# Layer 0's settings on GpSimd, its first heads later, and five smaller moves in a two-layer decoder trunk

## The chip, the cores and the metric

The kernel runs on one core of one Trainium2 chip. The core has TensorE (PE, with the weight load PEld shown apart), VectorE (DVE), ScalarE (ACT), GpSimd (POOL) and SyncE (SP, which issues most of the transfers). The metric is the device time of one execution in microseconds (us). Before the change it is 1268.68 us, the median of 3 runs (1268.33 to 1268.9).

## The reference

Two layers of a decoder trunk work on 512 tokens behind 16 learned meta tokens (528 columns), with a width of 1024, in float32. Each layer normalises, makes one projection for two groups of heads, transforms each group, joins them, projects back and adds; a SwiGLU block of width 2816 follows. Cut to what matters:

```python
def hybrid_layer(h, ...):
    xn = rmsnorm(h, attn_norm_g)
    fq, fk, fv, flog, rq, rk, rv, rg = split(xn @ w_in)
    logf = log_sigmoid(flog + b_fgate)                  # forget gates
    fox_out = fox_attention(fq, fk, fv, logf)           # 8 heads of 64:
        # c = cumsum(logf); softmax(q.k/8 + c[t] - c[s], s <= t) @ v
    rq, rk = rotate(rq), rotate(rk) / sqrt(128)
    ret = retention_chunkwise(rq, rk, rv)               # 4 heads of 128:
        # o_t = sum over s <= t of gamma^(t-s) (q_t.k_s) v_s
    ret = head_groupnorm(ret, ret_gn_g)                 # mean and variance of a head
    mix = concat([fox_out, silu(rg) * ret])
    h = h + mix @ w_out
    hn = rmsnorm(h, ffn_norm_g)
    return h + (silu(hn @ w_gate) * (hn @ w_up)) @ w_down
# after two layers: rmsnorm, and the 16 meta tokens are dropped
```

## The kernel before, in words

**Layout.** Activations lie transposed: 8 tiles of 128 features by 528 columns. A product in float32 is made of three matmuls on rounded parts: each weight tile is cast on ScalarE (whi, line 199), the remainder is subtracted on GpSimd or VectorE (wlo, line 202), the activations have xh and xl (lines 327 and 328), and TensorE adds whi·xh, whi·xl and wlo·xh in a bank (line 225). One such group for one of the 8 tiles is a "dense step": six matmuls of 264 columns in layer 0 (two halves of 528). Later results are split in the same way on ScalarE and VectorE (lines 150 and 151).

**Stages.** Layer 0's start fills fixed parts of tiles (`enter_att`, with `zero`, lines 91 and 122): one rows of the query tiles qo, zero rows of the key tiles kc, of the forget sums fs, the scores pr, the values pd, and small tiles pm and re. TensorE runs nine matmuls on ones until the first weights are there. Then come the norm of the layer, the first heads' projections, and the heads: four pairs of attention heads (`fox`) and four retention heads (`ret`, called hd 0 to 3).

An attention pair goes through scores (line 524: kc·qo with the forget sums in the same tile, and kx·qs), a masked maximum (line 528, nmax), the exponential on ScalarE (line 541), transposes on TensorE (line 427) into pth and ptl, and the product with the values (lines 586 and 594), which ScalarE and VectorE bring back with the sums (lines 588, 589, 597 and 598, into mixt).

A retention head goes through its values (transposed on TensorE, mean and centred values sq in lines 690 and 691, then rvh and rvl), rotated queries and keys (rqh, rql, rkh, rkl), scores (line 727), a product with the decay (line 732, sd), rounding into rsh and rsl, the product with the values (lines 758 and 761), the norm over the head (`col_rstd`: matmuls on ones in line 298, Ln and Exp in lines 303 and 304, one Newton step in lines 305 to 308) and the gate. For hd 0 and 1 the gate's silu is made from exponentials, which begins with a maximum with −80 (line 664, ge); for hd 2 and 3 it is the activation itself, whose table ScalarE must load (lines 416 and 418).

**Order.** TensorE's order is written out: a plan of steps, in which dense steps are the base, and the heads' steps are merged in at places counted in dense steps. `spread(main, a, b)` puts an attention pair's steps evenly between two places; `ret_places` takes ten numbers for a retention head's steps (the first for the values, the fourth and fifth for the first product and the third group of scores). The other engines' orders are made by a scheduler which keeps the dependencies; `pin` keeps a piece of work in the order of the program, `tc.high_priority()` lets it go ahead, and `tc.issue_after(x)` holds it behind x. Every engine carries out its own queue in order. Two tables of banks serve the matmuls: psd, and psa, whose banks a reader must leave before the next matmul takes them.

**The end.** The last norm works on two halves of columns. In the second half (`square_b`, `sum_b`, `after_7`) the squares of the 8 tiles are made on ScalarE (line 1140), six of them are added on VectorE (line 1143), and TensorE adds the sum and the last two squares by matmuls on ones (line 1169). Ln, Exp, a Newton step, the scaling and the last transfers follow.

Of the kernel before, what the change touches and what calls it, by code (L numbers as in the profile page):

```python
# [13 lines left out]
ALU = mybir.AluOpType  # L14
# [25 lines left out]
def hybrid_kernel(ctx, tc, x_t, w_in, w_fl, w_out, w_gate, w_up, w_down, vecs, b_fg, rope, decay, mask, ident, out_t):  # L40
# [42 lines left out]
    def enter_att(l):  # L83
# [37 lines left out]
    def zero(l, t):  # L121
        (nc.gpsimd if l else nc.vector).memset(t, 0.0)  # L122

# [166 lines left out]

    def col_rstd(parts, n, cols, rname, pinned=False):

# [6 lines left out]
        with tc.high_priority():  # L299
            r = tt(rname)  # L300
            a = tt("nwt")
            for v, (c0, c1) in zip(views, cols):
                pin(nc.scalar.activation(r[:, c0:c1], v, AF.Ln, bias=epsc, scale=1.0 / n), pinned)
            pin(nc.scalar.activation(r[:, c_all], r[:, c_all], AF.Exp, scale=-0.5), pinned)
            nc.vector.tensor_mul(a[:, c_all], r[:, c_all], r[:, c_all])
            for v, (c0, c1) in zip(views, cols):
                nc.vector.scalar_tensor_tensor(a[:, c0:c1], v, n * EPS, a[:, c0:c1], ALU.add, ALU.mult)
            nc.vector.scalar_tensor_tensor(r[:, c_all], a[:, c_all], 3.0 * n, r[:, c_all], ALU.subtract, ALU.mult)
# [6 lines left out]
    def pin(f, pinned=True):  # L315
        if pinned:
            tc.keep_in_program_order(f)

    def scale_split(st, gcol, cols, then=None):
# [3 lines left out]
        for k in range(NK):  # L323
            xh = state.tile([128, T], F32R, name=f"xh{k}", tag=f"xh{k}")
            xl = state.tile([128, T], F32R, name=f"xl{k}", tag=f"xl{k}")
            g = vcol(gcol + k)
            pin(nc.scalar.activation(xh[:, c], h[k][:, c], AF.Copy, scale=g), then)  # L327
            pin(nc.vector.scalar_tensor_tensor(xl[:, c], h[k][:, c], g, xh[:, c].bitcast(F32),  # L328
# [47 lines left out]
    def forget_gates(l, st):  # L376
# [251 lines left out]

    def ret_dense(l, hd, ly, real, st, which):
        QC = REAL if real else FULL  # L630
# [22 lines left out]
        def g_done(ps):  # L653
# [3 lines left out]
            if hd > 1:  # L657
                silu(sv(sg, real), LOGS)
                return
# [3 lines left out]
            x = sv(sg, real)  # L663
            nc.vector.scalar_tensor_tensor(u, x, -80.0, x, ALU.max, ALU.max)
            nc.scalar.activation(u, u, AF.Exp, scale=-1.0)
# [10 lines left out]
    def ret_steps(l, hd, st, real):  # L676
# [27 lines left out]
        def scores(grp):  # L704
# [26 lines left out]
            for kn, o, sc, dd in reads:  # L731
                nc.vector.tensor_mul(sd[0:kn, o], sc, dec[0:kn, dd])
# [92 lines left out]
    def ffn(l, st, real, last):  # L825
# [40 lines left out]
        def x_forms(k):  # L866
            def go():
# [4 lines left out]
                g0, g1 = vcol(V_FFN + l * NK + k), vcol(V_FFN + l * NK + HB + k)  # L872
                nc.scalar.activation(s[:, 0:2], two(h[k]), AF.Copy, scale=g0)
                nc.vector.tensor_sub(s[:, 2], s[:, 1], s[:, 0])
# [220 lines left out]
        else:  # L1095
# [34 lines left out]
            def square_b(m):  # L1130
                if m == 0:
                    t = fft("S", F32, (128, 6, w), 2)
                    fin["one"] = [t[:, i, 0:nb] for i in range(2)]
                    fin["acc"], fin["rb"], fin["tb"] = (t[:, i, 0:nb] for i in range(3, 6))
                    d = fin["acc"]
                elif m < NK - 2:
                    fin["sq", m] = d = tt("sq")[:, 0:nb]
                else:
                    d = fin["one"][m - NK + 2]
                pin(nc.scalar.activation(d, h[m][:, cb], AF.Square))  # L1140
# [111 lines left out]
    def layer(l):  # L1252
# [17 lines left out]
        def rd(hd, which):  # L1270
            return ret_dense(l, hd, ly, real, ret[hd], which)

# [42 lines left out]
        def first_parts():  # L1315
            ly["parts"] = col_parts(ly["acc"], FULL, True)
            convert(3, NK, True)
# [123 lines left out]
```

## Time and profile before

| | before |
|---|---|
| median of 3 runs | 1268.68 us |
| profiled execution | 1268.51 us |
| its span | 1266.7 us |
| TensorE busy | 1250.7 us (99%) |
| VectorE busy | 994.4 us (79%) |
| ScalarE busy | 706.2 us (56%) |
| GpSimd busy | 274.3 us (22%) |
| granted TensorE clock | 0.998 |

A row of a timeline gives the start, the duration, the engine, the line, the instruction, its output and inputs with their sizes, and in brackets how long the engine stood idle before it and what released it. "x2" is two instructions that follow each other. A row of the waits gives who waited for whom, the total in us, how many times, and the longest. The ends of matmuls are modelled, so times from start to start are used for TensorE where a tenth of a microsecond matters. A row of the stretches gives its limits and length, and for each engine the busy time and the number of instructions, then the granted clock, the transfers' share and GB/s.

### The profile page before, as it was taken

To read this page: it belongs to the slowest core of one execution; us is meant where nothing else is said; L and a number is where in the kernel's file an instruction comes from. 1 tells how busy PE (TensorE), PEld (TensorE's weight loads), DVE (VectorE), ACT (ScalarE), POOL (GpSimd) and SP (SyncE) were. 2 spreads that over 40 slices of the span, in tenths; PEclk is the share of its full clock that TensorE was granted. 3 is DMA by queue.
4 is the path that set the end of the run, shared out by engine and by line. 5 is a ranking of instruction groups with operands and counts; after the bars stand their busy time and mean duration, and the time that the engine had idled before them with its cause. 6 is when DMAs were issued, how large, how long until landed. Compare 5 with 4: busy or idle time off the path is not lost.

```text
span 1266.7 us, 23528 instructions
## 1 busy us (share of the span) xinstructions
PE 1250.7 (99%) x9223; PEld 1192.2 (94%) x9223; DVE 994.4 (79%) x1800; ACT 706.2 (56%) x1305; POOL 274.3 (22%) x540
## 2 busy tenths in 40 slices
PE   9999999999999999999999999999999999999997
PEld 9999999999999999999999989998789999999996
DVE  8887756879988888887786877567899888888867
ACT  7767655676444444444466665557764444444445
POOL 3555546420000000000126556554100000000000
PEclk9999999999999999999999999999999999999999
DMA  6212222223333333332322122222233333333321
GB/s 218 67 60 69 83 76 73 71 67 117 105 97 100 100 101 100 101 101 84 101 77 84 61 84 74 71 89 67 100 96 121 100 101 101 100 101 101 100 84 67
DMA packets 43342, 116.19 MB, mean 92 GB/s; under 512 B 5088, under 2 KB 12000, under 8 KB 43232
## 3 DMA queue, kind: packets, MB, share of 16 engines
q1 hardware_dynamic: 42800, 114.41, 28.1%
q8 instruction: 72, 1.18, 0.4%
q14 instruction: 38, 0.31, 0.1%
q10 hardware_dynamic: 432, 0.29, 0.1%
HBM read 112.58 MB, written 2.10 MB: 91 GB/s over the span
## 4 chain that ended last, share of the span: by engine, by line
PE 91%; DVE 4%; ACT 4%; issue 1%; DMA 0%; ACTq 0%; DVEq 0%
PE psd L225 28%; PE psa L912 18%; PE psd L1047 14%; PE psd L912 13%; PE psa L225 5%; PE psa L1047 4%; PE psa L427 2%; PE psa L524 1%; PE psa L594 1%; PE psa L761 1%; PE psa L727 1%; ACT whi L199 1%; PE psa L298 0%; ACT xh L327 0%; DMA raw<-w_in 0%
## 5 line engine op out<-in xcount | busy, mean ns | idle before, releaser
L202 POOL TENSOR_TENSOR wlo<-raw,whi 128x128 fp32r<-128x128 f32 x504 | 259.1, 548 | 256.0 <-ACT whi L199 235.3
L225 PE MATMUL psd<-xh,whi 128*128 128x264 f32 (+1 forms) x792 | 195.5, 314 | 0.0
L225 PE MATMUL psd<-xh,wlo 128*128 128x264 f32 (+1 forms) x792 | 186.9, 304 | 0.0
L225 PE MATMUL psd<-xl,whi 128*128 128x264 f32 (+1 forms) x792 | 186.4, 303 | 0.4 <-DVE xl L328 0.4
L225 PEld LDWEIGHTS psd<-xh,whi 128*128 128x128 f32 x792 | 128.5, 190 | 4.9 <-ACT whi L199 0.5
L225 PEld LDWEIGHTS psd<-xh,wlo 128*128 128x128 f32 x792 | 127.0, 188 | 6.3 <-DVE wlo L202 0.4
L225 PEld LDWEIGHTS psd<-xl,whi 128*128 128x128 f32 x792 | 127.6, 189 | 5.1 <-DVE xl L328 1.1
L199 ACT CAST whi<-raw 128x512 fp32r<-128x512 f32 (+1 forms) x168 | 97.9, 613 | 41.7 <-PE psd L225 28.6
L900 ACT CAST whi<-raw 128x1024 fp32r<-128x1024 f32 (+2 forms) x62 | 54.8, 885 | 51.2 <-PE psd L912 39.8
L900 ACT CAST fwhi<-raw 128x1024 fp32r<-128x1024 f32 (+2 forms) x62 | 55.6, 897 | 48.0 <-PE psd L912 40.5
L122 POOL MEMSET kc<- 64x528 f32 x2 | 1.1, 532 | 345.4 <-PE psa L912 345.4
L901 DVE TENSOR_TENSOR wlo<-raw,whi 128x1024 fp32r<-128x1024 f32 (+2 forms) x62 | 62.9, 1015 | 12.6 <-ACT whi L900 12.5
L901 DVE TENSOR_TENSOR fwlo<-raw,fwhi 128x1024 fp32r<-128x1024 f32 (+2 forms) x62 | 64.0, 1033 | 11.0 <-ACT fwhi L900 10.7
L912 PE MATMUL psa<-th,whi 128*128 128x264 f32 (+1 forms) x232 | 65.4, 282 | 0.0
L912 PE MATMUL psa<-th,wlo 128*128 128x264 f32 (+1 forms) x232 | 65.4, 282 | 0.0
L912 PE MATMUL psa<-tl,whi 128*128 128x264 f32 (+1 forms) x232 | 65.3, 282 | 0.0
L912 PE MATMUL psa<-th,fwhi 128*128 128x264 f32 (+1 forms) x224 | 63.4, 283 | 0.0
L912 PE MATMUL psa<-tl,fwhi 128*128 128x264 f32 (+1 forms) x224 | 63.3, 283 | 0.0
L912 PE MATMUL psa<-th,fwlo 128*128 128x264 f32 (+1 forms) x224 | 63.2, 282 | 0.0
L541 ACT ACTIVATE pr<-pr,nmax 128x144 f32<-128x144 f32 (+1 forms) x64 | 36.8, 575 | 44.4 <-DVE nmax L528 25.7
L900 ACT CAST fwhi<-S 128x1024 fp32r<-128x1024 f32 x20 | 21.0, 1049 | 68.6 <-PE psa L912 66.5
L978 ACT COPY e<-psa 128x264 f32<-128x264 f32 (+1 forms) x114 | 42.9, 376 | 28.3 <-PE psa L912 24.1
(368 smaller groups left out, 4044.8 us busy)
## 6 DMA issues: line engine op xcount, KB each, us to landing
raw<-w_in SPq DMA_DIRECT2D x54, 512.0 KB, 3.5
raw<-w_gate SPq DMA_DIRECT2D x44, 512.0 KB, 4.0
fraw<-w_up SPq DMA_DIRECT2D x38, 512.0 KB, 3.5
raw<-w_down SPq DMA_DIRECT2D x64, 256.0 KB, 2.9
raw<-w_out SPq DMA_DIRECT2D x16, 512.0 KB, 3.5
raw<-w_down SPq DMA_DIRECT2D x32, 192.0 KB, 2.5
raw<-w_up SPq DMA_DIRECT2D x6, 512.0 KB, 3.5
h<-x_t SPq DMA_DIRECT2D x8, 264.0 KB, 4.5
```

Source lines behind the costliest of these rows:

```text
L199: pin(nc.scalar.copy(hi, job["raw"][:, c0:c1]), pinned)
L202: pin(sub(lo[:, c:c + step], job["raw"][:, c0 + c:c0 + c + step], hi[:, c:c + step].bitcast(F32)), pinned)
L225: nc.tensor.matmul(ps[1][b][:, 0:c1 - c0], w[:, wk, :], x[:, c0:c1], start=(k == 0 and i == 0), stop=(k == n - 1 and i == 2))
L427: nc.tensor.transpose(ps[:, 128 * j:128 * j + 128], src[:, o:o + 128], idt)
L524: nc.tensor.matmul(sc[0:nq, 0:c1 - c0], qq[:, q0:q0 + nq], kk[:, c0:c1], start=(i == 0), stop=(i == 1))
L541: nc.scalar.activation(pr, pr, AF.Exp, bias=nmax[0:nq], scale=-1.0, accum_out=rsum)
L594: nc.tensor.matmul(po[:, c0:SEQ], v[:, j, :], pp[:, j, META + c0:T], start=(j == 0 and i == 0), stop=(j == 4))
L900: nc.scalar.copy(hi, src)
L901: nc.vector.tensor_sub(lo, src, hi.bitcast(F32))
L912: nc.tensor.matmul(bank()[:, 0:b.shape[-1]], a[:, o + k, :], b, start=(fresh and k == 0 and i == 0), stop=(k == n - 1 and i == 2), skip_gr ...
L978: nc.scalar.copy(self.t["e"][:, i], self.t["x"][:, 0:w])
L1047: nc.tensor.matmul(v[:, 0:c1 - c0], a[:, s * n + k, :], b[:, c0:c1], start=(k == 0 and i == 0), stop=(k == n - 1 and i == 2))
```

## The change

Seven things change:

1. The twelve settings of zeros and ones of layer 0 that stood on VectorE are made on GpSimd, as those of layer 1 already were.
2. Places: in the first group of heads, layer 0's first attention pair goes from 11 to 12 (its end from 32.5 to 33), hd 0's values from 13 to 17.5 and its first product from 37.5 to 38.6 (38.3 in layer 1); hd 3's fifth place, the third group of its scores, goes from 55.5 to 54.9.
3. The gate's maximum with −80 is a `tensor_scalar_max` on one input instead of a `scalar_tensor_tensor` that names the same tile twice.
4. In layer 0's third retention head (hd 2) the norm's sums are copied from their banks by ScalarE, and the Newton step reads the copy.
5. The rounded scores rsh and rsl have three buffers instead of two; hd 3's last rounding goes ahead with priority, and hd 2's silu is issued after it. The first norm's rounding is now written out in `first_rounding`, and a copy of the forget gates is issued after it.
6. In layer 1 the second normalised forms of the FFN's inputs (S, line 873) are issued after the last xh.
7. At the end three squares instead of two go to TensorE's sum, and VectorE's last addition falls away.

```diff
-            (nc.gpsimd if l else nc.vector).memset(q_tiles[s][rest].bitcast(F32), 1.0)
+            nc.gpsimd.memset(q_tiles[s][rest].bitcast(F32), 1.0)
...
     def zero(l, t):
-        (nc.gpsimd if l else nc.vector).memset(t, 0.0)
+        nc.gpsimd.memset(t, 0.0)
...
+    def first_rounding(st):
+        c = slice(0, T)
+        sh, sl = st["parts"] = tt("sqh", F32R), tt("sql", F32R)
+        st["rounding"] = pin(nc.scalar.copy(sh[:, c], st["acc"][:, c])).ins
+        pin(nc.vector.tensor_sub(sl[:, c], st["acc"][:, c], sh[:, c].bitcast(F32)))
...
             for v, (c0, c1) in zip(views, cols):
                 pin(nc.scalar.activation(r[:, c0:c1], v, AF.Ln, bias=epsc, scale=1.0 / n), pinned)
+            if aside:
+                t = tt("sq")
+                for v, (c0, c1) in zip(views, cols):
+                    nc.scalar.copy(t[:, c0:c1], v)
+                views, cols = [t[:, c_all]], [(cols[0][0], cols[-1][1])]
...
-                nc.scalar.copy(z2[:, c0:c1], ps[32:32 + FH, 0:c1 - c0])
+                with ExitStack() if l else tc.issue_after(st["rounding"]):
+                    nc.scalar.copy(z2[:, c0:c1], ps[32:32 + FH, 0:c1 - c0])
...
-                silu(sv(sg, real), LOGS)
+                with tc.issue_after(other["rounded"]) if hd == 2 else ExitStack():
+                    silu(sv(sg, real), LOGS)
...
-            nc.vector.scalar_tensor_tensor(u, x, -80.0, x, ALU.max, ALU.max)
+            nc.vector.tensor_scalar_max(u, x, -80.0)
...
-            sh = at("rsh", bufs=2)
-            sl = at("rsl", bufs=2)
+            sh = at("rsh", bufs=3)
+            sl = at("rsl", bufs=3)
             full = used if kn == 128 else used - n
-            split(sh[:, 0:full], sl[:, 0:full], sd[:, 0:full])
+            with tc.high_priority() if hd == RH - 1 and grp[0] == 2 else ExitStack():
+                st["rounded"] = nc.scalar.copy(sh[:, 0:full], sd[:, 0:full]).ins
+                nc.vector.tensor_sub(sl[:, 0:full], sd[:, 0:full], sh[:, 0:full].bitcast(F32))
...
-            r = col_rstd(st["parts"], 128, QC, "r")
+            r = col_rstd(st["parts"], 128, QC, "r", aside=hd == 2 and not real)
...
-                nc.scalar.activation(s[:, 0:2], two(h[k]), AF.Copy, scale=g0)
+                with tc.issue_after(st["scaled"].ins) if real else ExitStack():
+                    nc.scalar.activation(s[:, 0:2], two(h[k]), AF.Copy, scale=g0)
...
-                    fin["one"] = [t[:, i, 0:nb] for i in range(2)]
+                    fin["one"] = [t[:, i, 0:nb] for i in range(3)]
...
-                elif m < NK - 2:
+                elif m < NK - 3:
...
-                sum_b(5)
                 v = psum_a()[:, 0:nb]
-                sums(v, [fin["one"][0], fin["acc"], fin["one"][1]])
+                sums(v, [fin["one"][0], fin["acc"]] + fin["one"][1:])
...
-            m0, r0, places = (((7 if l else 11, 31 if l else 32.5), (34, 40.5), (13, 33.5, 35.5, 37.5, 39, 40.5, 43, 44, 47.5, 48)),
+            m0, r0, places = (((7 if l else 12, 31 if l else 33), (34, 40.5), (13 if l else 17.5, 33.5, 35.5, 38.3 if l else 38.6, 39, 40.5, 43, 44, 47.5, 48)),
...
-                      ret_places(3, 52, 45.5, 47.5, 57.5, 55.5, 58.5, 60, 64.1, 63, 64.2))
+                      ret_places(3, 52, 45.5, 47.5, 57.5, 54.9, 58.5, 60, 64.1, 63, 64.2))
```

How this moves the instructions shows in the engines' orders. Line numbers after the change are larger by 12 to 17 from `first_rounding` on (the scores' line 524 is 538, the max's 664 is 679).

TensorE, where the first attention pair of layer 0 begins. Before:

```order
L225 MATMUL psd<-xh_181,whi 128x264 x2
L225 MATMUL psd<-xl_182,whi 128x264 x2
L225 MATMUL psd<-xh_181,wlo 128x264 x2
L524 MATMUL psa<-kc_105,qo_103 16x16
L524 MATMUL psa<-kx_462,qs_453 16x16
L225 MATMUL psd<-xh_185,whi 128x264 x2
```

And with the change:

```order
L225 MATMUL psd<-xh_181,wlo 128x264 x2
L225 MATMUL psd<-xh_185,whi 128x264 x2
L225 MATMUL psd<-xl_186,whi 128x264 x2
L225 MATMUL psd<-xh_185,wlo 128x264 x2
L538 MATMUL psa<-kc_105,qo_103 16x16
L538 MATMUL psa<-kx_462,qs_453 16x16
```

One dense step (xh_185, xl_186) has moved ahead of the first scores.

VectorE, around the first head's max (ge) late in the first group of layer 0; sg is the gate's input, pr and nmax the scores' maxima of the attention pair, ptl the transposed scores' remainder, sd the retention scores with their decay. Before:

```order
L655 SCALAR_TENSOR_TENSOR sg<-psd,R 128x528
L528 ISA pr,nmax<-psa,msk 128x264
L528 ISA nmax 128x1
L528 ISA pr,nmax<-psa,msk 128x264
L528 ISA nmax 128x1
L664 SCALAR_TENSOR_TENSOR ge<-sg 128x528
L533 TENSOR_TENSOR nmax<-nmax 128x1
L151 TENSOR_TENSOR ptl<-psa,pth 128x128
L545 STREAM_TRANSPOSE pe<-pr 32x128
L549 RECIPROCAL sums<-sums 128x8
L732 TENSOR_TENSOR sd<-psa,dec 128x264 x2
```

And with the change:

```order
L542 ISA pr,nmax<-psa,msk 128x264
L542 ISA nmax 128x1
L542 ISA pr,nmax<-psa,msk 128x264
L542 ISA nmax 128x1
L669 SCALAR_TENSOR_TENSOR sg<-psd,R 128x528
L547 TENSOR_TENSOR nmax<-nmax 128x1
L151 TENSOR_TENSOR ptl<-psa,pth 128x128
L679 TENSOR_SCALAR ge<-sg 128x528
L559 STREAM_TRANSPOSE pe<-pr 32x128
L563 RECIPROCAL sums<-sums 128x8
L747 TENSOR_TENSOR sd<-psa,dec 128x264 x2
```

The max is another instruction, and the correction of the maxima and ptl stand ahead of it; sd still stands behind it.

ScalarE, at the norm of layer 0's third retention head; ol is an attention pair's product on its way to mixt, rkh a rotated key's rounded part. Before:

```order
L303 ACTIVATE r<-psa,epsc 128x264
L588 COPY ol<-psa 64x16
L303 ACTIVATE r<-psa,epsc 128x264
L568 CAST pth<-pm 16x16
L304 ACTIVATE r<-r 128x528
L150 CAST rkh<-tq 128x528
L597 COPY ol<-psa 64x512
```

And with the change:

```order
L309 ACTIVATE r<-psa,epsc 128x264 x2
L313 COPY sq<-psa 128x264 x2
L315 ACTIVATE r<-r 128x528
L602 COPY ol<-psa 64x16
L611 COPY ol<-psa 64x512
L150 CAST rkh<-tq 128x528
L582 CAST pth<-pm 16x16
```

The two copies are new, the copies of ol stay ahead of rkh, and rkh comes behind both of them instead of between them.

More of the change, by code (lines that the diff above doesn't have):

```diff
@@ L326, in scale_split @@
             g = vcol(gcol + k)
-            pin(nc.scalar.activation(xh[:, c], h[k][:, c], AF.Copy, scale=g), then)
+            st["scaled"] = nc.scalar.activation(xh[:, c], h[k][:, c], AF.Copy, scale=g)
+            pin(st["scaled"], then)
             pin(nc.vector.scalar_tensor_tensor(xl[:, c], h[k][:, c], g, xh[:, c].bitcast(F32),
@@ L627, in hybrid_kernel, with ret_dense @@
     KLEN = (128, 128, 128, 128, META)
-    def ret_dense(l, hd, ly, real, st, which):
+    def ret_dense(l, hd, ly, real, st, which, other):
         QC = REAL if real else FULL
@@ L1132, in square_b @@
                     t = fft("S", F32, (128, 6, w), 2)
[L1133 removed]
+                    fin["one"] = [t[:, i, 0:nb] for i in range(3)]
                     fin["acc"], fin["rb"], fin["tb"] = (t[:, i, 0:nb] for i in range(3, 6))
                     d = fin["acc"]
[L1136 removed]
+                elif m < NK - 3:
                     fin["sq", m] = d = tt("sq")[:, 0:nb]
                 else:
[L1139 removed]
+                    d = fin["one"][m - NK + 3]
                 pin(nc.scalar.activation(d, h[m][:, cb], AF.Square))
@@ L1270, in rd @@
         def rd(hd, which):
-            return ret_dense(l, hd, ly, real, ret[hd], which)
+            return ret_dense(l, hd, ly, real, ret[hd], which, ret[RH - 1])
         mixes = [[fox[0], ret[0], fox[1], ret[1]], [fox[2], ret[2], fox[3], ret[3]]]
```

5 lines of the change are left out of this document (3 added, 2 removed).

## The prediction

> **What bounds the kernel now.** I read the page first (busy times, then the chain that ended last), then the waits of TensorE, then its busy time by stretches, then the timeline around every wait of TensorE that these showed.
>
> ```profile
> PE 1250.7 (99%) x9223; PEld 1192.2 (94%) x9223; DVE 994.4 (79%) x1800; ACT 706.2 (56%) x1305; POOL 274.3 (22%) x540
> ...
> PE 91%; DVE 4%; ACT 4%; issue 1%; DMA 0%; ACTq 0%; DVEq 0%
> ```
>
> TensorE (PE) works 1250.7 us of a span of 1266.7. The other 4% + 4% of the chain are the places at which it stood still. The change touches no matmul but one, so it can only win back the remaining 16 us of idle time or add to them. The waits of TensorE name their pieces:
>
> ```profile
> PE psa L1283 <- DVE wide L62: 1.6, 1, 1.6
> PE psa L727 <- DVE ptl L151: 1.0, 1, 1.0
> PE psa L761 <- DVE rsl L151: 0.9, 3, 0.4
> PE psa L1169 <- ACT S L1140: 0.9, 1, 0.9
> PE psa L524 <- DVE kc L472: 0.8, 1, 0.8
> PE psa L594 <- DVE ptl L151: 0.7, 1, 0.7
> PE psa L524 <- DVE mixt L598: 0.7, 1, 0.7
> PE psa L427 <- DVE sd L732: 0.4, 1, 0.4
> PE psa L524 <- DVE sq L691: 0.4, 1, 0.4
> PE psd L225 <- DVE xl L328: 0.4, 1, 0.4
> PE psa L761 <- ACT rsh L150: 0.2, 1, 0.2
> PE psa L427 <- DVE nmax L528: 0.2, 1, 0.2
> ```
>
> Total us, times, longest: 8.2 us in fourteen waits; the rest of the 16 is the tail after the last matmul. By stretches (length, then busy time and count of PE, PEld, DVE, ACT, POOL, then clock):
>
> ```profile
> 36.00:75.00 39.00, 35.04 (x274) 33.04 (x273) 30.95 (x85) 25.66 (x68) 16.34 (x34) 1.00 0.19 65
> 75.00:230.00 155.00, 155.00 (x1268) 154.12 (x1266) 109.73 (x271) 97.61 (x239) 89.16 (x172) 1.00 0.23 74
> 230.00:265.00 35.00, 34.30 (x272) 33.57 (x271) 26.49 (x59) 25.47 (x54) 13.91 (x27) 1.00 0.19 61
> ```
>
> So 39.00 − 35.04 = 3.96 us of idle time lie between 36 and 75 us, where the first heads of layer 0 run. These are eight of the fourteen waits (kc, nmax, sq, product ptl, score ptl, sd, rsh, one rsl). A full stretch issues 1268 matmuls in 155 us, one every 0.122. A wait costs more than its idle time, since a matmul's end counts as busy:
>
> ```profile
> 36.40 0.40 PE L225 MATMUL psd<-xh,wlo 128*128 128x264 f32 x2
> 37.56 0.17 PE L524 MATMUL psa<-kc,qo 128*16 128x16 f32 x1 [0.76 <-DVE kc L472]
> ```
>
> The second matmul of that pair starts 0.122 after 36.40, the next one at 37.56: 1.04 where 0.12 is dense, a loss of 0.92 against 0.76 shown. I add 0.16 to each wait: 3.96 + 8 × 0.16 = 5.2 us are lost between 36 and 75.
>
> **The change part by part.** I take times from the profiled execution, 1268.51 us (span 1266.7 and 1.8 around it); the median of the runs is 1268.68, 0.17 more.
>
> Twelve settings on GpSimd. VectorE's queue loses them ahead of its first x form:
>
> ```profile
> 1.72 0.50 DVE L122 MEMSET kc<- 64x528 f32 x1 [0.16 <-issue]
> ...
> 5.53 0.73 DVE L328 SCALAR_TENSOR_TENSOR xl<-h,vec,xh 128x528 fp32r<-128x528 f32 x1
> ```
>
> The settings fill VectorE from 1.72 until 5.53, so xl comes up to 1 us sooner. Of that TensorE can use little, about 0.3 us: its first product waits for whi as well. And 0.3 us won there only lengthens the wait for kc, which ends at 37.41 (37.56 on TensorE) after a chain on ScalarE and VectorE. I count 0; the bounds are −0.3 and +0.3. GpSimd is free for them: its own few settings are short, and its subtractions start much later.
>
> First heads later. One dense step (6 matmuls of 264 columns, 6 × 0.122 = 0.73 us) goes ahead of the first scores, which wait for kc. At 37.56 TensorE has done 0.73 us more: +0.73. The values of the first retention head go from place 13 to 17.5, so the score that waited for the bank freed by sq L691 (0.4 + 0.16) and the transposes that waited for nmax (0.2 + 0.16) find theirs free: +0.9. But TensorE now comes 1.6 us sooner to the first transposes of pr and to the product that waits for ptl L151, while VectorE's row of score maxima, vv and the two passes over the values stays as long, only in another order. By VectorE's new order I lay the score maxima at about 47.2 where TensorE arrives at about 46.7, an estimate from the durations before: a new wait of 0.7. The product's wait (0.7 + 0.16) shrinks by about half: +0.4. Sum for 36 to 58 us: 0.73 + 0.9 − 0.7 + 0.4 = 1.3. Bounds: 0 (all is waited for again) and 0.73 + 0.9 + 0.9 = 2.5.
>
> The max of the gate, one input instead of two, and behind the first score correction:
>
> ```profile
> 62.55 3.72 DVE L664 SCALAR_TENSOR_TENSOR ge<-sg 128x528 f32<-128x528 f32 x1
> 66.19 0.15 DVE L533 TENSOR_TENSOR nmax<-nmax 128x1 f32<-128x1 f32 x1
> 66.26 0.28 DVE L151 TENSOR_TENSOR ptl<-psa,pth 128x128 fp32r<-128x128 f32 x1
> ...
> 68.13 1.20 DVE L732 TENSOR_TENSOR sd<-psa,dec 128x264 f32<-128x264 f32 x3
> ```
>
> ```profile
> 62.32 3.38 POOL L202 TENSOR_TENSOR wlo<-raw,whi 128x128 fp32r<-128x128 f32 x8
> ```
>
> ```profile
> L664 DVE SCALAR_TENSOR_TENSOR ge<-sg x4: 658/795/3722, 62.5 to 750.2; 128x528 f32<-128x528 f32 x2, 128x512 f32<-128x512 f32 x2
> ```
>
> ```profile
> L472 DVE TENSOR_SCALAR kc<-fs,pick x2: 490/535/580, 36.9 to 665.6; 40x528 fp32r<-40x528 f32 x2
> ```
>
> The first of four L664 took 3.72 us, against a shortest of 0.66. It started 0.23 after eight subtractions of GpSimd in a row and ended 0.57 after the last (65.70): it did not run beside them. Behind it stood nmax and ptl, which TensorE waited for (1.0 + 0.16), then sd (0.4 + 0.16), and through these rsh (0.2 + 0.16) and rsl ((0.9 − 0.4) / 2 = 0.25 of the row of three, + 0.16): 2.5 us together. In the new order nmax and ptl are issued before the max, and the max is a one-input instruction. Nearest row: L472, 0.49 to 0.58 on the same 528 columns; the other bound is 3.72 again. I take 0.5, since nothing with one tensor input stood as long in this trace: all four waits go, +2.5. If the max is held as long as before it costs what the second rival says.
>
> The Trainium skill bears on this, against the change. "SBUF — State Buffer", "SBUF: two separate sides", says that VectorE and GpSimd share one pair of ports as an exclusive lock for a whole instruction, and that VectorE asks for it with two SBUF inputs or in a two-port mode. The 3.72 beside the eight subtractions agrees. "VectorE: DVE Perf Modes", "Mode 2×_2P", gives the two-port mode to single-source fp32 instructions from SBUF; by it the new max would need the lock as well, which is the second rival's case. No run here shows that yet.
>
> Third norm's sums copied. Two ScalarE copies of 264 columns and one VectorE instruction of 528 in place of two:
>
> ```profile
> L978 ACT COPY e<-psa x114: 356/374/382, 324.0 to 1225.3; 128x264 f32<-128x264 f32 x57, 128x256 f32<-128x256 f32 x57
> ```
>
> ```profile
> L307 DVE SCALAR_TENSOR_TENSOR nwt<-psa,nwt x19: 413/432/692, 25.4 to 924.2; 128x264 f32<-128x264 f32 x14, 128x512 f32<-128x512 f32 x5
> ```
>
> ```profile
> 239.48 0.28 PE L524 MATMUL psa<-kx,qs 128*128 128x264 f32 x1
> 240.47 0.39 PE L524 MATMUL psa<-kc,qo 128*128 128x264 f32 x1 [0.70 <-DVE mixt L598]
> ```
>
> ```profile
> 239.74 0.67 DVE L598 TENSOR_TENSOR mixt<-psa,ol 64x512 f32<-64x512 f32 x1
> ```
>
> ```profile
> 234.37 4.88 POOL L202 TENSOR_TENSOR wlo<-raw,whi 128x128 fp32r<-128x128 f32 x8 [4.16 <-ACT whi L199]
> ```
>
> The scores at 240.47 waited 0.70 for a bank that L598 read until 240.41. With the sums copied, two banks of the norm are free when the second copy ends, some 2 × 0.374 after the norm's second Ln, at about 237.6, ahead of TensorE at 239.6; those scores stop waiting: 0.70 + 0.16 = 0.86. The copies and the reordering put rkh and rkl some 1.2 us later, and the products with them (L727, 241.54) would come 0.86 sooner: I lay rkl at about 241.0 against 240.7 and leave 0.35 of a wait. +0.5; bounds 0.9 and, if the new two-input instruction is held by GpSimd like L664, the third rival.
>
> Three buffers for rounded scores, and the last rounding of the fourth head with priority:
>
> ```profile
> 880.01 1.28 ACT L418 ACT_TABLE_LOAD   x1
> ...
> 882.29 0.54 ACT L150 CAST rsh<-sd 128x416 fp32r<-128x416 f32 x1
> ```
>
> In layer 1 this rounding stands behind two table loads of 1.28 and TensorE's earlier product, whose buffer it takes. It now goes first, so one wait for rsl of the three (0.4 + 0.16, at 882.9) goes: +0.56. What it is moved past is a whi cast, a silu and two mxh casts, each up to 0.9 later; mxh is used by TensorE some 4 us on. A second rsl wait (701 us, about 0.28 + 0.16) goes, because layer 1's first product stands one dense step later: +0.44.
>
> Layer 1's FFN start. Two casts stood ahead of the last x form's:
>
> ```profile
> 911.04 1.33 ACT L873 ACTIVATE S<-h,vec 128x512 f32<-128x512 f32 x2
> 912.28 0.71 ACT L327 ACTIVATE xh<-h,vec 128x512 fp32r<-128x512 f32 x1
> ```
>
> They are now issued behind it. That x form comes 1.3 us sooner and the wait for xl (0.4 + 0.16) goes: +0.56. The differences that read S begin only after eight subtractions on VectorE, so their delay is covered.
>
> The end. One VectorE addition of squares less, one pair of matmuls more.
>
> ```profile
> 1256.95 0.68 ACT L1140 ACTIVATE S<-h 128x240 f32<-128x240 f32 x2
> ```
>
> ```profile
> 1257.39 1.48 PE L1169 MATMUL psa<-S,ones 128*128 128x240 f32 x6 [0.89 <-ACT S L1140]
> ```
>
> Three pairs of matmuls took 1.48, so a further pair some 0.4. TensorE waited 0.89 for the first of these two squares; it can now start with the one before, some 0.6 sooner. +0.2, bounds −0.2 and +0.4.
>
> Sum: 1.3 + 2.5 + 0.5 + 0.56 + 0.44 + 0.56 + 0.2 = 6.1. 1268.51 − 6.1 = 1262.4; with the 0.17 of the median, **1262.6 us**. That the early gain is kept: from 75 to 230 TensorE is busy 155.00 of 155.00, with GpSimd at 89 and VectorE at 110, so nothing there is shorter of time than TensorE.
>
> **The rivals.**
>
> *The stage stays as long.* VectorE is busy 30.95 of the 39 us from 36 to 75, ScalarE 25.66, with waits between them; TensorE would only come sooner to the same results. For it: six of the eight waits there are for VectorE's results one after the other, and the change gives VectorE almost nothing to save but the max. Against it: the 3.1 us of the held L664 are themselves on that row. Then the 3.8 of this stage fall out, and 2.3 stay: 1266.4.
>
> *The max is held again.* The eight subtractions still follow one another for 3.4 us, now also around the max. Then sd, behind it, comes about 0.8 us earlier than 68.13 and no more, since ptl no longer waits for the max but sd does. Everything gained before is waited for there: 0.8 in place of 3.8, so 1268.5 − 0.8 − 2.3 + 0.2 = 1265.6. For it: the 3.72 us. Against it: the one-input rows of 0.49 to 0.58.
>
> *GpSimd's row holds VectorE at both new places, and the kernel gets slower.* L307's one-instruction form in the third norm now reads two SBUF inputs, sq and nwt, as L664 did; from the bank it took 0.41 to 0.69. Behind it in VectorE's queue stands rkl, for which TensorE waits. If it starts inside a row of eight subtractions like the one of 4.88 us that ended at 239.25, it stands up to 3.0 longer (3.72 − 0.7), with the 0.5 lost. With the second rival's loss: 1268.5 − 0.8 − 1.76 + 3.0 + 0.2 = 1269.1. It decides where more than 2.6 us of subtractions remain when that instruction starts. Against it: it starts at about 239.5, after that row's end.
>
> That the change doesn't do what it says: the new orders show every move, so I give this no share.
>
> **How the numbers follow.** My forecast, all waits but those named gone: 0.60. Max held again: 0.17. Stage as long: 0.13. Both held: 0.05. What I have not seen (a wait at a new place): 0.05, to both sides. The low end: all of 5.2 + 0.86 + 0.56 + 0.44 + 0.56 + 0.4 = 8.0 won, 1260.6, a little less for an earlier start: 1260.3. The high end takes in the first two rivals: 1266.6. The likeliest case alone spans 1260.3 to 1264. A measurement of this kernel tells 0.2%, 2.5 us, from no change: faster means below 1266.1. Forecast, held max and half of what is unseen: 0.79. Same: the unchanged stage and the third rival's smaller prices, 0.16. Slower: 0.05.
>
> **What would show it.** In the changed kernel's waits: ptl before L727 and sd gone, kc still there with 0.5 to 0.8, a wait for nmax at about 46 us; TensorE's busy time from 36 to 75 at least 37 of 39; the first max near 0.5 us; the score at 240 not waiting for L598; the fourth head's 416-column rounding before the table loads; the xl wait at 914 gone. The prediction is wrong if the max takes over 2 us, if 36 to 75 still shows over 3 us of idle time, or if a stretch that was full (75 to 230, 265 to 640, 930 to 1250) shows idle time.

## The result, and the profile after

The change takes 1261.31 us (median of 6 runs, 1261.24 to 1262.03) against 1268.58 before (6 runs, 1268.33 to 1268.9): 0.9944 of the time, 95% interval 0.9931 to 0.9956. That is 7.3 us less; 6.1 were forecast.

The page of the changed kernel, TensorE's share first and then the chain that ended last by engine:

```profile
PE 1248.7 (99%) x9225; PEld 1191.9 (95%) x9225; DVE 989.2 (79%) x1786; ACT 706.6 (56%) x1307; POOL 281.6 (22%) x552
...
PE 95%; DVE 3%; ACT 2%; DMA 0%; issue 0%; ACTq 0%; DVEq 0%
```

TensorE's share of the chain went from 91% to 95%. Its waits, in the same columns as before:

```profile
PE psa L1300 <- DVE wide L62: 1.6, 1, 1.6
PE psa L608 <- DVE ptl L151: 0.5, 1, 0.5
PE psa L1187 <- ACT S L1158: 0.2, 1, 0.2
PE psa L441 <- DVE nmax L542: 0.2, 1, 0.2
PE psd L225 <- DVE xl L341: 0.2, 1, 0.2
```

(Lines 538, 608, 1187 and 1300 are 524, 594, 1169 and 1283 of before; the offset goes from 6 in `col_rstd` to 18 at the end.) Fourteen waits have become five. The wait for kc is gone, as are the waits for sq, sd, rsh, rsl, mixt, and the score's wait for ptl. The wait for xl in this list is another one, at 7.7 us in the kernel's start; the one at 914 us (now 908) no longer shows. By stretches:

```profile
36.00:75.00 39.00, 38.21 (x307) 37.25 (x306) 32.87 (x91) 29.48 (x78) 20.05 (x39) 1.00 0.21 69
...
230.00:265.00 35.00, 34.91 (x277) 34.14 (x277) 28.70 (x60) 25.83 (x52) 16.72 (x32) 1.00 0.14 46
```

Between 36 and 75 us TensorE issues 307 matmuls, where it issued 274. The stretch from 930 to 1250, full before, now has 0.21 us of idle time: the wait for S, which has moved ahead of 1250 with the end. Taken from start to start (the time between two matmuls over that of a dense row), the 7.1 us by which the span is shorter come from these places:

| place | lost before, us | lost after, us | gain, us | forecast, us |
|---|---|---|---|---|
| first scores (kc), with the dense step done ahead | 37.56 | 37.26, and 0.73 of work more | 1.03 | 0.73 |
| 40 to 58 us (nmax, sq, product) | 0.36 + 0.60 + 0.96 | 0.36 + 0.78 | 0.78 | 0.6 |
| 65 to 71 us (ptl, sd, rsh, rsl) | 1.13 + 0.60 + 0.36 + 0.51 | 0 | 2.60 | 2.5 |
| about 239, and 247 after | 0.86 | 0.34 | 0.52 | 0.5 |
| 259 and 701 (rsl) | 0.15 + 0.44 | 0 | 0.59 | 0.44 |
| 882.9 (rsl), and 880 after | 0.67 | 0.24 | 0.43 | 0.56 |
| 914 (xl and the next matmul) | 0.56 + 0.14 | 0.19 | 0.51 | 0.56 |
| last dense matmul to the end | 10.49 | 10.23 | 0.26 | 0.2 |

These are 6.7 us; the other 0.4 lie scattered in rows that were dense already. By size each term came out near its forecast. Whether it came from the edit to which the forecast ascribed it is what the experiments ask. The largest is the row of 65 to 71 us. VectorE of the changed kernel there, and then GpSimd:

```profile
60.76 0.69 DVE L669 SCALAR_TENSOR_TENSOR sg<-psd,R 128x528 f32<-128x528 f32 x1
61.38 0.50 DVE L547 TENSOR_TENSOR nmax<-nmax 128x1 f32<-128x1 f32 x1
61.80 0.27 DVE L151 TENSOR_TENSOR ptl<-psa,pth 128x128 fp32r<-128x128 f32 x1
62.00 0.42 DVE L679 TENSOR_SCALAR ge<-sg 128x528 f32<-128x528 f32 x1
```

```profile
60.52 3.90 POOL L202 TENSOR_TENSOR wlo<-raw,whi 128x128 fp32r<-128x128 f32 x8
```

The max (ge) takes 0.42 us in the middle of GpSimd's eight subtractions, and these now take 3.90 us where they took 3.38: this time GpSimd waited for VectorE. All of that lies in the fourth subtraction, which takes 0.95 us (61.78 to 62.73) where 0.45 is usual, while VectorE does nmax, ptl and the max one after the other. That looks like the forecast, a one-input max that isn't held. The experiments say otherwise.

### The profile page after: what moved, and what is told of

It is laid out like the page before. It is cut to its first block, busy times and chain, and to the rows that moved or that the text cites. A ratio compares the mean times of both kernels' runs of the same rounds, so it can differ in the third digit from the quotient of the medians.

```text
span 1259.6 us, 23534 instructions
## 1 busy us (share of the span) xinstructions
PE 1248.7 (99%) x9225; PEld 1191.9 (95%) x9225; DVE 989.2 (79%) x1786; ACT 706.6 (56%) x1307; POOL 281.6 (22%) x552
## 4 chain that ended last, share of the span: by engine, by line
PE 95%; DVE 3%; ACT 2%; DMA 0%; issue 0%; ACTq 0%; DVEq 0%
PE psd L225 31%; PE psa L930 18%; PE psd L1065 14%; PE psd L930 13%; PE psa L225 5%; PE psa L1065 4%; PE psa L441 2%; PE psa L608 2%; PE psa L538 1%; PE psa L742 1%; PE psa L778 1%; PE psa L402 1%; PE psa L304 0%; DMA raw<-w_in 0%; PE psa L617 0%
## 5 line engine op out<-in xcount | busy, mean ns | idle before, releaser
L202 POOL TENSOR_TENSOR wlo<-raw,whi 128x128 fp32r<-128x128 f32 x504 | 262.4, 555 | 243.0 <-ACT whi L199 220.9
L918 ACT CAST whi<-raw 128x1024 fp32r<-128x1024 f32 (+2 forms) x62 | 54.9, 885 | 51.3 <-PE psd L930 39.8
```

Source lines behind the costliest of these rows:

```text
L202: pin(sub(lo[:, c:c + step], job["raw"][:, c0 + c:c0 + c + step], hi[:, c:c + step].bitcast(F32)), pinned)
L918: nc.scalar.copy(hi, src)
```

## The experiments

Each kernel was timed in five rounds. The kernel before stood at 1268.5 to 1268.7 in these rounds, so the medians are set against the change's 1261.31 or against before, as said. I take differences below about 0.3 us to tell nothing. Two pieces of the change were not undone by themselves: the written-out first rounding with the held copy of the forget gates (item 5), and hd 3's place 54.9 (item 2).

### The max with two inputs, in its new place

```diff
-            nc.vector.tensor_scalar_max(u, x, -80.0)
+            nc.vector.scalar_tensor_tensor(u, x, -80.0, x, ALU.max, ALU.max)
```

> The changed kernel with the gate's maximum as the two-input form of before, in its new place behind nmax and ptl. Theory (two SBUF inputs are shut out by GpSimd's row of subtractions): the first max takes about 3 us, up to some 0.6 us after the eighth subtraction (64.4 in the changed kernel), sd behind it comes about 2 us later than 63.27, and the kernel takes 1.5 to 2.2 us more than the 1261.3 of the change. Rival (the new place alone cured it): the max stays under 0.8 us and the time within 0.3 us of the change.

Measured: 1261.57 us, ratio to before 0.9944 (0.9931 to 0.9956). VectorE, and GpSimd behind it:

```profile
61.58 0.50 DVE L547 TENSOR_TENSOR nmax<-nmax 128x1 f32<-128x1 f32 x1
62.01 0.27 DVE L151 TENSOR_TENSOR ptl<-psa,pth 128x128 fp32r<-128x128 f32 x1
62.22 0.69 DVE L679 SCALAR_TENSOR_TENSOR ge<-sg 128x528 f32<-128x528 f32 x1
```

```profile
60.73 4.18 POOL L202 TENSOR_TENSOR wlo<-raw,whi 128x128 fp32r<-128x128 f32 x8
```

The two-input max takes 0.69 us inside the row; it isn't held. The theory that two inputs are what is shut out falls.

### The max as a plain two-tensor instruction

```diff
-            nc.vector.tensor_scalar_max(u, x, -80.0)
+            nc.vector.tensor_tensor(u, x, x, ALU.max)
```

> The same, with the maximum as a plain two-tensor instruction of the gate's input with itself (the lower bound of -80 is left out). Theory (any two SBUF inputs): as the two-input form, about 3 us. Rival (only the scalar_tensor_tensor form is held so long, as the two-tensor subtractions of the trace were held 0.1 to 0.5 us): the max takes about 0.7 to 1.2 us and the time is within 0.5 us of the change.

Measured: 1261.63 us, 0.9944 (0.9932 to 0.9957), the max at 0.69 us. The same answer: in the changed kernel the form of this instruction is worth nothing that can be told.

### The one-input max alone

```diff
 (the kernel before)
-            nc.vector.scalar_tensor_tensor(u, x, -80.0, x, ALU.max, ALU.max)
+            nc.vector.tensor_scalar_max(u, x, -80.0)
```

> The kernel before with the one-input maximum and nothing else. Theory: the first max takes 0.4 to 0.5 us in place of 3.72, and the waits for ptl (L727), sd, rsh and rsl between 65 and 71 us go: 2 to 2.5 us less than before, some 1266.2. Rival (VectorE's row sets this stage and TensorE only arrives sooner at the next result): under 1 us less.

Measured: 1268.14 us, 0.9994 (0.9985 to 1.0003): no difference from before that can be told. VectorE, then GpSimd:

```profile
62.49 3.45 DVE L664 TENSOR_SCALAR ge<-sg 128x528 f32<-128x528 f32 x1
65.86 0.15 DVE L533 TENSOR_TENSOR nmax<-nmax 128x1 f32<-128x1 f32 x1
```

```profile
62.26 3.38 POOL L202 TENSOR_TENSOR wlo<-raw,whi 128x128 fp32r<-128x128 f32 x8
```

The one-input max is held as long as the other one: it ends 0.3 us after the eighth subtraction (62.26 + 3.38 = 65.64) instead of 0.57, which is the difference of the two forms' own durations (0.42 and 0.69). So neither form is proof against the hold, and neither brings it.

### The places of before

```diff
-            m0, r0, places = (((7 if l else 12, 31 if l else 33), (34, 40.5), (13 if l else 17.5, 33.5, 35.5, 38.3 if l else 38.6, 39, ...
+            m0, r0, places = (((7 if l else 11, 31 if l else 32.5), (34, 40.5), (13, 33.5, 35.5, 37.5, 39, ...
...
-                      ret_places(3, 52, 45.5, 47.5, 57.5, 54.9, ...
+                      ret_places(3, 52, 45.5, 47.5, 57.5, 55.5, ...
```

> The changed kernel with the places of before (first pair 11, values 13, first product 37.5, fifth place of the last head 55.5). Theory: the waits for kc (0.73), the bank of sq (0.6), nmax (0.36) and, in layer 1, rsl at 701 us (0.44) come back, and the two waits of the change between 46 and 57 us (1.1) shrink: 1 to 2 us more than the change. Rival (the stage is as long as VectorE's row): within 0.5 us of the change.

Measured: 1264.95 us, 0.9971 (0.996 to 0.9983) of before: 3.6 us more than the change, nearly twice the most that the theory allowed. TensorE's row from 36 to 75 us, and the max of this kernel:

```profile
36.00:75.00 39.00, 35.78 (x278) 33.67 (x277) 31.19 (x86) 26.29 (x72) 17.22 (x36) 1.00 0.21 65
```

```profile
62.43 3.04 DVE L679 TENSOR_SCALAR ge<-sg 128x528 f32<-128x528 f32 x1
```

kc, nmax, sq and the product lose 0.96 + 0.31 + 0.59 + 0.96 here, where the change loses 0.22 + 0.36 + 0.78: 1.5 us, near the 1.3 that the forecast gave the places. But the hold is back as well, with ptl, sd, rsh and rsl (0.67 + 0.35 + 0.36 + 0.51 = 1.9 us). The wait for rsl at 700 us is back with 0.16 alone, where the theory had 0.44. With the old places VectorE's order has the max ahead of nmax again. The next run asks whether that order decides.

### The max behind nmax and ptl, in the kernel before

The max is issued later and held behind the remainder ptl; it keeps two inputs.

```diff
 (the kernel before)
...
+                with tc.issue_after(mark["ptl"]) if l == 0 and hd == 0 else ExitStack():
+                    nc.vector.scalar_tensor_tensor(u, x, -80.0, x, ALU.max, ALU.max)
...
```

> The kernel before with its two-input maximum held behind nmax and the first ptl on VectorE, as the changed kernel's order has it; nothing else on purpose (three neighbours of the same head follow in another order). Theory, after the one-input maximum alone was still held for 3.45 us: the place, not the kind, decides. Then ptl comes at about 62.9, the wait of 1.0 for it before L727 goes, and with it sd, rsh and rsl: 1.5 to 2.5 us less than before. Rival (the held maximum only moves: it stands as long in its new place, now ahead of sd): the ptl wait goes, sd's grows, under 0.8 us less.

Measured: 1268.03 us, 0.9994 (0.9985 to 1.0003) of before. VectorE, then GpSimd:

```profile
63.57 3.06 DVE L534 TENSOR_TENSOR nmax<-nmax 128x1 f32<-128x1 f32 x1
66.55 0.28 DVE L575 TENSOR_TENSOR ptl<-psa,pth 128x128 fp32r<-128x128 f32 x1
66.75 0.69 DVE L671 SCALAR_TENSOR_TENSOR ge<-sg 128x528 f32<-128x528 f32 x1
```

```profile
63.23 3.38 POOL L203 TENSOR_TENSOR wlo<-raw,whi 128x128 fp32r<-128x128 f32 x8
```

Now nmax, an instruction on 128 single numbers that takes 0.15 us in the kernel before, takes 3.06, and the max behind it 0.69. What is held is whichever of the two comes first, not a kind. It isn't any instruction, though: sg and the masked maxima, which read a bank, ran beside this row undelayed (sg 0.69 us in the changed kernel, inside the row). Neither the place in the order nor the form of the max removes the hold.

### The row of GpSimd taken away

The eight subtractions of this row (the job with the number 8) go to VectorE, as two instructions; the max keeps its form and place.

```diff
 (the kernel before)
-        sub = nc.gpsimd.tensor_sub if job["pool"] else nc.vector.tensor_sub
+        pool = job["pool"] and j != 8
+        sub = nc.gpsimd.tensor_sub if pool else nc.vector.tensor_sub
...
-            step = 1 if job["pool"] else c1 - c0
+            step = 1 if pool else c1 - c0
```

> The kernel before, with the eight subtractions that follow GpSimd's copy of kc at 61.65 given to VectorE as two of 128x512 (behind ptl in its order); the maximum keeps its form and place. Theory (GpSimd's unbroken row holds VectorE's first instruction on the shared memory path, whatever it is): the maximum takes 0.66 to 0.7 us in place of 3.72, ptl comes at about 63.4, and of the waits for ptl, sd, rsh and rsl between 65 and 71 us (2.6) at least 1.5 go: 1.5 to 2.3 us less than before, though VectorE has 1.4 us more to do. Rival (the maximum is held by something else, or the stage is as long as VectorE's row): the maximum stays over 2 us, or the time within 0.7 us of before.

Measured: 1266.31 us, 0.9981 (0.9973 to 0.999) of before, 2.4 us less. VectorE, and the stretch from 36 to 75:

```profile
62.50 0.71 DVE L665 SCALAR_TENSOR_TENSOR ge<-sg 128x528 f32<-128x528 f32 x1
63.12 0.15 DVE L534 TENSOR_TENSOR nmax<-nmax 128x1 f32<-128x1 f32 x1
63.19 0.28 DVE L151 TENSOR_TENSOR ptl<-psa,pth 128x128 fp32r<-128x128 f32 x1
63.39 1.28 DVE L203 TENSOR_TENSOR wlo<-raw,whi 128x512 fp32r<-128x512 f32 x2
```

```profile
36.00:75.00 39.00, 36.82 (x294) 35.64 (x293) 31.89 (x92) 28.44 (x76) 15.10 (x30) 1.00 0.22 72
```

Without the row the same max takes 0.71 us, and all four waits between 65 and 71 us are gone, though VectorE has 1.28 us more to do. So without GpSimd's row there is no hold, and 2.4 us is its price in the kernel before.

### The settings back on VectorE

```diff
-            nc.gpsimd.memset(q_tiles[s][rest].bitcast(F32), 1.0)
+            (nc.gpsimd if l else nc.vector).memset(q_tiles[s][rest].bitcast(F32), 1.0)
...
-        nc.gpsimd.memset(t, 0.0)
+        (nc.gpsimd if l else nc.vector).memset(t, 0.0)
```

> The changed kernel with layer 0's twelve settings back on VectorE. Prediction's reading: 0, since a later first product only shortens the wait for kc. Rival, after the first scores of the changed kernel began 0.30 us sooner and without a wait for kc: the start and the kc chain are later by the same amount, 0.3 to 0.6 us more than the change.

Measured: 1263.3 us, 0.9956 (0.9944 to 0.9969) of before: 2.0 us more than the change, beyond both. VectorE and GpSimd late in the first group:

```profile
62.44 2.54 DVE L547 TENSOR_TENSOR nmax<-nmax 128x1 f32<-128x1 f32 x1
64.90 0.28 DVE L151 TENSOR_TENSOR ptl<-psa,pth 128x128 fp32r<-128x128 f32 x1
65.10 0.42 DVE L679 TENSOR_SCALAR ge<-sg 128x528 f32<-128x528 f32 x1
```

```profile
61.58 3.38 POOL L202 TENSOR_TENSOR wlo<-raw,whi 128x128 fp32r<-128x128 f32 x8
```

The hold is back, on nmax, until the row's end. Its waits (0.50 + 0.20 + 0.67, start to start) make 1.4 of the 2.0 us. The remaining 0.6 would fit the start: the first scores come at 38.30 here and at 37.26 in the changed kernel. But this point moves from execution to execution: in the profiles of the other kernels with the new places and the settings on GpSimd it lies between 37.14 and 37.61, and once at 38.08. The profiled execution is also the slowest of the five, 0.7 us above their median. So 0.6 for the start is not shown. The order of the instructions from 36 to 75 us is that of the changed kernel; only the settings moved.

### The sums not copied

```diff
-            r = col_rstd(st["parts"], 128, QC, "r", aside=hd == 2 and not real)
+            r = col_rstd(st["parts"], 128, QC, "r", aside=False)
```

> The changed kernel without the copies of the third norm's sums. Theory: the wait of the scores for mixt (L612 of the changed kernel) near 238 us is back with 0.86 us, and the wait of 0.33 for ptl at 247 may go: 0.4 to 0.9 us more than the change. Rival (the bank is not what the scores wait for any more): within 0.2 us.

Measured: 1262.27 us (1261.84 to 1262.6), 0.9946 (0.9933 to 0.996), 1.0 us more than the change. The wait is back with 0.86 from start to start, and the 0.33 at 247 us is gone, which makes 0.53; the profiled execution of 1262.6 also reached its first scores 0.8 later, some 200 us ahead of the third norm.

The wait in this kernel:

```profile
PE psa L538 <- DVE mixt L612: 0.7, 1, 0.7
```

### Two buffers, no priority, silu not held

```diff
-            sh = at("rsh", bufs=3)
-            sl = at("rsl", bufs=3)
+            sh = at("rsh", bufs=2)
+            sl = at("rsl", bufs=2)
...
-            with tc.high_priority() if hd == RH - 1 and grp[0] == 2 else ExitStack():
+            with ExitStack():
...
-                with tc.issue_after(other["rounded"]) if hd == 2 else ExitStack():
+                with ExitStack():
```

> The changed kernel with two buffers for rsh and rsl, without the priority of the last rounding and without the silu held behind it. Theory: the waits for rsl at about 255 (0.15) and 876 us (0.67) are back, the new one of 0.24 near 880 goes: 0.5 to 0.8 us more than the change. Rival (the last rounding is reached in time by the other moves): within 0.2 us.

Measured: 1262.91 us, 0.9951 (0.9939 to 0.9964), 1.6 us more than the change. Two waits for rsl are back, and there is one for rsh:

```profile
PE psa L778 <- DVE rsl L753: 0.5, 2, 0.2
PE psa L778 <- ACT rsh L752: 0.2, 1, 0.2
```

From start to start they cost 0.45 at 254 us, and 0.39 + 0.50 at 877 us, against 0.24 that go: 1.1 us. The profiled execution took 1262.55, 1.2 more than that of the change, so the waits account for it; the further 0.4 of the median are not explained. By the trace this part is worth up to twice what the forecast gave it, and the trace shows why: at 877 us TensorE waits for the rounding itself (rsh) too, where the kernel before waited for its remainder alone.

### S ahead of the last x form

```diff
-                with tc.issue_after(st["scaled"].ins) if real else ExitStack():
+                with ExitStack():
```

> The changed kernel without holding S behind the last xh of layer 1's FFN. Prediction's reading: the wait for xl near 908 us is back with 0.56 where the change shows 0.19: 0.3 to 0.5 us more than the change. Rival: within 0.15 us.

Measured: 1261.87 us, 0.9946 (0.9934 to 0.9959), 0.6 more than the change. The wait is 0.4 again, in place of 0.0 at this point of the changed kernel (0.55 and 0.19 from start to start, so 0.36 of the 0.6):

```profile
PE psd L225 <- DVE xl L341: 0.4, 1, 0.4
```

### The old end

```diff
-                    fin["one"] = [t[:, i, 0:nb] for i in range(3)]
+                    fin["one"] = [t[:, i, 0:nb] for i in range(2)]
...
+                sum_b(5)
                 v = psum_a()[:, 0:nb]
-                sums(v, [fin["one"][0], fin["acc"]] + fin["one"][1:])
+                sums(v, [fin["one"][0], fin["acc"], fin["one"][1]])
```

> The changed kernel with the end of before: two squares and the sum to TensorE, and the last addition on VectorE. Prediction's reading: 0.2 us more than the change (wait for S 1.06 instead of 0.38, one pair of matmuls of 0.41 less). Rival: the addition was on the chain, 0.4 us or more.

Measured: 1261.82 us, 0.9945 (0.9933 to 0.9958), 0.5 more. The wait for S is 0.9 again:

```profile
PE psa L1187 <- ACT S L1158: 0.9, 1, 0.9
```

By the medians the rival's 0.4 or more would hold. The trace speaks for the forecast: from the last dense matmul to the end it takes 10.51 us, against 10.23 in the change, 0.3 us more. That is near the limit of what can be told.

### The values later still

```diff
-            ... (13 if l else 17.5, 33.5, 35.5, 38.3 if l else 38.6, ...
+            ... (13 if l else 19, 33.5, 35.5, 38.3 if l else 38.6, ...
```

> An attempt at less: the changed kernel with the first retention head's values at place 19 in place of 17.5, which puts the maxima of the second scores ahead of the means on VectorE. Theory: the wait for nmax at 46 us (0.36) goes, and the rest stays: 0.2 to 0.4 us less than the change. Rival: ptl of the product, now behind rkl on VectorE, is later and the wait at 56 us (0.78) grows by up to 0.7: 0 to 0.5 us more than the change; and if the timing at GpSimd's row shifts, VectorE may be held there again, 1 to 2 us more.

Measured: 1261.37 us, 0.9941 (0.9928 to 0.9955): as the change. The wait for nmax at 46 us is gone and the product's has grown:

```profile
PE psa L608 <- DVE ptl L151: 0.7, 1, 0.7
PE psa L1187 <- ACT S L1158: 0.2, 1, 0.2
```

From start to start 0.36 went, 0.15 came at the product and 0.19 at 51 us. That fits the prediction's first rival in small: VectorE's row sets this piece, and TensorE waits for it at one point or another.

## Why the prediction was right, and where it wasn't

The time lay inside the range, 1.3 us below the forecast of 1262.6, and the sum of the terms (6.1) stands against 7.3 measured. Most of the smaller terms were right in cause and near in size. The largest, the max, was right in size by luck. Point by point:

**The settings** (counted 0). The step "0.3 us won there only lengthens the wait for kc" holds where TensorE does wait for kc: with the settings on GpSimd and the old places the first scores came at 37.46, with a wait of 0.80, against 37.56 and 0.76 before. It fails together with the new places, which the prediction did not consider: with one dense step more ahead, TensorE hardly waits there, and what it gains at the start counts. So one sign that the prediction named, a wait for kc of 0.5 to 0.8 that stays, did not come. In the changed kernel:

```profile
36.80 0.40 PE L225 MATMUL psd<-xh,wlo 128*128 128x264 f32 x2
37.26 0.17 PE L538 MATMUL psa<-kc,qo 128*16 128x16 f32 x1
```

The first scores follow the last dense matmul at 36.92 by 0.34, where 0.12 is dense. 0.3 us of the gain stand here, no more than this point moves between executions. The settings had a second effect, which nothing in the prediction provided for: without their move VectorE is held again (1.4 us).

**The first heads later** (+1.3 for 36 to 58 us). Right in size as a sum (1.03 + 0.78 with the settings' 0.3, and 1.5 by the run with the old places), and right in that a new wait for nmax comes and the product's wait stays in part. Two errors cancelled: the wait for nmax is 0.36 from start to start where 0.7 was forecast, and the product's shrank from 0.96 to 0.78, not by half to 0.43.

**The max** (+2.5). The size was right, 2.60, and the cause was wrong; that the two met is luck. The step "the max is a one-input instruction ... nothing with one tensor input stood as long in this trace" failed: the one-input max alone was held for 3.45 us and gained nothing that can be told, the two-input max in the changed kernel was not held, and with another order nmax was held for 3.06. The row L664 of before was read rightly ("it did not run beside them", GpSimd's subtractions), which the run without the row showed. What was not seen is that the hold belongs to the encounter of VectorE with that row, and not to the max. Of the profiles taken, five show it (before; the max alone; the old places; the max behind ptl; the settings back), and the changed kernel and its seven other variants don't; the fourteenth has no such row. Which it is, is settled neither by form nor by order: the settings' run has the changed kernel's order there and is held.

What does decide stays open. In the changed kernel nmax starts 0.02 us into the third subtraction (61.36) and gets in after it; with the settings back it starts as far into the third (62.41) and waits for the last; without the copied sums it starts as far into the third again (62.19) and gets in. So the moment within the subtraction does not tell them apart. Everywhere else in these traces VectorE waited for the subtraction that was running, at most about 0.35 us, and then got in. That GpSimd's eight follow each other without a pause is not enough either. In the kernel before itself the second head's max, of the same form and size, met such a row and was not held:

```profile
121.23 0.66 DVE L664 SCALAR_TENSOR_TENSOR ge<-sg 128x528 f32<-128x528 f32 x1
```

```profile
120.79 4.42 POOL L202 TENSOR_TENSOR wlo<-raw,whi 128x128 fp32r<-128x128 f32 x8 [1.57 <-ACT whi L199]
```

The row of 62 us also follows GpSimd's copy of kc without a pause, with both of its weight halves cast by then, in the changed kernel (60.52) as before; whether that helps the hold was not tried.

The Trainium skill, "SBUF — State Buffer", section "SBUF: two separate sides", lets the shared pair of ports be held for a whole instruction. The usual 0.35 us agrees with that; the five holds of 2.4 to 3.1 us go beyond it, over up to eight instructions of 0.45, so the prediction's word that the 3.72 us agree was too much. What the prediction drew from the Trainium skill, "VectorE: DVE Perf Modes", "Mode 2×_2P", that a single-source fp32 instruction takes both ports too, agrees with the 3.45 us of the one-input max, and the prediction weighed it too lightly.

**The copied sums** (+0.5): right, 0.52 in the trace and 0.53 at the same two waits when undone (1.0 in the medians). The forecast's remaining wait came as 0.34, though at the next product (ptl at 247 us), not for rkl.

**Three buffers, S, the end, the rsl wait of layer 1** (0.56, 0.56, 0.2, 0.44): 0.43, 0.51, 0.26, 0.44 in the trace. The buffers were worth 1.6 when undone (1.1 by the waits). For the last one, the rsl wait at 701 us, the prediction named the place alone, and the max has a part in it: with the one-input max and the old places the wait is 0.15 (the max alone) and 0.16 (the old places), with the two-input max and the new places there is none. Either move would have removed most of it.

**The rivals.** "The max is held again" did not come about in the changed kernel. The two variants that are held (old places, settings back) show that it could have, but not as laid out: with the settings back nmax is held and TensorE waits for ptl too, and what was gained before is not all waited for. The price is 1.9 and 1.4 us, where I took 3.0. "The stage stays as long" fell: 38.21 of 39 us. The slower rival did not come about: the third norm's instruction on two inputs stood beside no row (it starts at 234.84 us, GpSimd's row had ended at 234.55).

The undone parts add up to more than 7.3 us (3.6 + 2.0 + 1.0 + 1.6 + 0.6 + 0.5 + 0.3 = 9.6). The hold is paid in two of them (1.9 and 1.4); the rest of the excess is not explained.

## What to carry to other kernels

A single instruction far above its kind's usual time may be a fact about a meeting of two engines, as here, and not about that instruction: change its form, its place and the other engine one at a time before ascribing the gain. Where an independent step removes such a meeting by a small shift in time, the gain is real and can be lost again by any other edit that shifts it; taking the other engine's row away removed it here (2.4 us) at the cost of its work. When all the waits of the bounding engine are summed with what they cost from start to start, the sum can come near the whole even where a single cause is wrong, as it did here; such a sum is no proof of its causes.

## What the runs showed of the hardware that was not expected

VectorE can be held by GpSimd for a whole row of eight instructions (3.38 us) and not just for one; it was so in five profiles of the thirteen that have the row. The held instruction may be of one or two inputs and as small as 128x1 (3.06 us where 0.15 is usual). In the other eight the two met with 0.35 us of delay for VectorE, and one subtraction of GpSimd stood instead until VectorE's nmax, ptl and max were done (0.95 us with the one-input max, 1.23 with two inputs, where 0.45 is usual). The outcome was the same in all rounds of a kernel, as far as the narrow spread of the times tells (1261.24 to 1262.03 for the change, 1263.12 to 1263.97 with the settings back).
